# Tree attention on one core: transposes one pair ahead at first, V copies spread by pairs, loads in another order

## The chip, the cores and the metric

The kernel runs on one NeuronCore of a Trainium2 chip. The metric is the device time of one execution in microseconds (us); smaller is better. The core's engines run at the same time, each through its own instructions in order: TensorE (PE, matmuls and transposes; PEld is its weight load), VectorE (DVE), ScalarE (ACT), GpSimd (POOL) and SyncE (SP). Data moves between the device memory (HBM) and the on-chip memory by DMAs, which one of the engines issues and which 16 DMA engines then carry out.

## The reference

```python
def setup_inputs():
    batch, heads, seq, dim = 8, 12, 512, 64          # Q, K, V: float32, random normal
...
def reference(Q, K, V):
    scale = 1.0 / np.sqrt(dim)
    mask = np.zeros((seq, seq))
    for i in range(seq):                 # a row attends to itself and its ancestors
        mask[i, i] = 1                   # in a binary heap
        parent = i
        while parent > 0:
            parent = (parent - 1) // 2
            mask[i, parent] = 1
    scores = np.einsum('bhqd,bhkd->bhqk', Q, K) * scale
    scores = scores + (1 - mask) * (-1e9)
    weights = np.exp(scores - np.max(scores, axis=-1, keepdims=True))
    weights = weights / (np.sum(weights, axis=-1, keepdims=True) + 1e-10)
    return np.einsum('bhqk,bhkd->bhqd', weights, V).astype(np.float32)
```

Batch and heads are taken together: 96 heads of 512 rows by 64 columns.

## The kernel before

Heads are worked on in pairs, 48 of them (pair i is heads 2i and 2i+1), and loaded in groups of 8 heads (12 groups, four pairs each). Row 4p+t of a head lies in partition p, slot t.

**One pair.** `transpose(i)` (L254) turns the pair's K and Q by 16 matmuls into one PSUM tile `kqp`, of which there is a single buffer. `evac(i)` (L267) copies it to `kq` on DVE, a pair's K and Q side by side. `scores1` (L283) and `scores2` (L305) each add a mask code to the scores by matmuls over `ctile` and then multiply keys and queries from `kq`; ACT takes the exponential of each (L298, L321). `values(i)` (L337) multiplies the weights with V from the tile `vt`, into a single PSUM buffer `ob`, with a column of ones that gives the sums. `norm(i)` (L369) takes the reciprocal of the sums and multiplies, both on DVE, into `of`.

**V copies.** `values` needs V in an order of rows that follows the tree. Three kinds of copies bring it from the loaded tile `vst` into `vt`, all recorded at L209: `spread_l7` on DVE (32 partitions, two slots), `spread_top` (32 partitions, one slot) on POOL, for the first four heads on DVE, and `spread_leaves` (64 partitions, two slots) on ACT or POOL. A group takes 4 + 4 + 2 of them; early groups are taken by halves of 4 heads. `early_copies(i)` is the table of what is copied at step i up to 11; from 12 on, the group after the current one is copied, one `spread_l7` and a share of the others per step. `spread(i)` issues them, and from step 6 on makes the first POOL copy behind a DVE copy of the same step wait for that DVE copy (`after`, L390).

**Loads.** All loads but the first pair's K and Q are issued by POOL (L189), in its program order, between its copies; they read float32 and write bfloat16. `loads_at(i)` says which are issued after step i's copies: eleven before the loop, then those of its table, and from step 13 on three in four steps. The K and Q tiles and the V tiles have four buffers each, one per group in flight. A DMA issued by POOL counts on one of eight semaphores by turns, and the compiled program makes a DMA wait until the one eight places before it has landed. Stores of finished groups (1 MB, L385) are issued by POOL from step 33 on, one a step, the last group's in three pieces.

**The order of the steps** is written out by hand in the loop at L496; no scheduler moves anything. At step i PE does the scores of pair i, then `values(i - 1)`, then the transposes of pair i+2 (`AHEAD` makes exceptions of steps 1 to 3, where two pairs are transposed at once or none). Before the loop stand eight matmuls over zeros (`fill`), the first pair's transposes and scores, five more `fill` matmuls, the second pair's transposes, the copies of the first four heads' V and `values(0)`.

Of the kernel before, what the change touches and what calls it, by code (L numbers as in the profile page):

```python
# [98 lines left out]
def kernel(  # L99
# [12 lines left out]
    NH = B * H  # L112
    NP = NH // 2
# [100 lines left out]
    def spread_top(eng, j, g, h0=0, h1=GB):  # L214
        return copy(
            eng, vtile(g)[32 * j:32 * j + 32, h0:h1, 0, 0:D],
            vsts[g][0:32, h0:h1, UNITS[TOP + j][1], :],
        )

    def spread_leaves(eng, r, g, h0=0, h1=GB):  # L220

        p = 64 if r else 0
        return copy(
            eng, vtile(g)[p:p + 64, h0:h1, 1 + r:4 + r:2, 0:D],
            vsts[g][64:128, h0:h1, r:3 + r:2, :],
        )
# [27 lines left out]
    def transpose(i):  # L254
        kqp = psT.tile([P, 2, 32, 32], bf16, name="kqp")
        kqps[i] = kqp
        for t in range(4):
            for a in range(2):
                transpose_one(kqp[:, 0, :, :], i, a, t, _slot_layout(t)[1], ksts, perms[t])
        for x, t in enumerate(ORDER):  # L260
            for a in range(2):
                transpose_one(
                    kqp[:, 1, :, :], i, a, t, [2 * x, 2 * x + 1, 2 * x + 9, 2 * x + 10],
                    qsts, qperm,
                )

    def evac(i):  # L267
        kq = work.tile([P, 2, 16, 32], bf16, name="kq")
        kTs[i] = kq[:, 0, :, :]
        qTs[i] = kq[:, 1, :, :].rearrange("p (t u) c -> p t (u c)", t=4)  # L270
        src = kqps[i][:, :, 0:18, :]
        src = bass.AP(
            src.tensor, src.offset,
            [list(src.ap[0]), [1024, 2], [32, 8], [9 * 32, 2], [1, 32]],
        )
        nc.vector.tensor_copy(  # L276
            out=kq[:, :, :, :].rearrange("p k (x y) c -> p k x y c", y=2), in_=src
        )
# [48 lines left out]
    def fill(i, n):  # L327

        if i not in obs:
            obs[i] = psO.tile([P, 2, 512], fp32, name="ob")  # L330
        for k in range(n):
            nc.tensor.matmul(
                out=obs[i][:, k % 2, :], lhsT=zeros[:, 0:128], rhs=zeros[:, :],
                start=True, stop=True,
            )

    def values(i):  # L337

        if i == NP - 1:
            obs[i] = psT.tile([P, 2, 512], fp32, name="kqp")  # L340
        elif i not in obs:
            obs[i] = psO.tile([P, 2, 512], fp32, name="ob")
        ob = obs[i]
        e1, e2, vt = ets[i], e2s[i % NE], vtile(2 * i // GB)

        def product(e, a, t, tile_v, lo=0, hi=128, **flags):
            nc.tensor.matmul(  # L347
                out=ob[lo:hi, a, 65 * t:65 * t + 65],
                lhsT=e[:, a, PLACE[t], lo:hi],
                rhs=vt[:, 2 * i % GB + a, tile_v, 0:D + 1],  # L350
                **flags,
            )

        def first(a):
            for t in range(4):
                product(e1, a, t, 0, start=t == 0, stop=False)
            for t in (2, 3):
                product(e2, a, t, 1 + t, start=False, stop=False)

        def second(a):  # L360
            for t in (0, 1):
                product(e2, a, t, 1 + SELF[t], 0, 64, start=False, stop=t == 1)
                product(e2, a, t, 1 + t, 64, 128, start=False, stop=t == 1)

        order = (first, second) * 2 if i == NP - 1 else (first, first, second, second)
        for n, part in enumerate(order):
            part(n // 2 if i == NP - 1 else n % 2)

    def norm(i, heads=((0, 2),)):  # L369
        g, r = divmod(i, 4)  # L370
        if r == 0:
            ofs[g] = opool.tile([P, GB, 4, D], fp32, name="of")
        for a0, a1 in heads:
            o4 = obs[i][:, a0:a1, 0:260].rearrange("p a (t c) -> p a t c", c=D + 1)
            rec = small.tile([P, a1 - a0, 4, 1], fp32, name="rec")
            nc.vector.reciprocal(out=rec[:, :, :, :], in_=o4[:, :, :, D:D + 1])  # L376
            nc.vector.tensor_tensor(  # L377
                out=ofs[g][:, 2 * r + a0:2 * r + a1, :, :],
                in0=o4[:, :, :, 0:D],
                in1=rec[:, :, :, :].to_broadcast([P, a1 - a0, 4, D]),  # L380
                op=ALU.mult,
            )
# [15 lines left out]

    def early_copies(i):

        def l7(g, js, *h):
            return [(spread_l7, DVE, j, g) + h for j in js]

        def top(g, js, *h):
            return [(spread_top, POOL, j, g) + h for j in js]

        def leaf(eng, g, rs, *h):
            return [(spread_leaves, eng, r, g) + h for r in rs]

        every = range(4)  # L410
        return {
            0: l7(0, every, 0, 4) + [(spread_top, DVE, j, 0, 0, 4) for j in every]
            + leaf(ACT, 0, (0, 1), 0, 4),
            1: l7(0, every, 4, 8) + top(0, every, 4, 8) + leaf(ACT, 0, (0, 1), 4, 8),
            3: l7(1, every, 0, 4) + top(1, every, 0, 4) + leaf(ACT, 1, (0, 1), 0, 4),
            5: l7(1, every, 4, 8) + top(1, every, 4, 8) + leaf(ACT, 1, (0, 1), 4, 8),
            6: l7(2, (0,)) + top(2, (0, 1)) + leaf(ACT, 2, (0,)),
            7: l7(2, (1, 2)) + top(2, (2, 3)) + leaf(ACT, 2, (1,)),
            8: l7(2, (3,)),
            9: l7(3, (0,)) + top(3, (0, 1)),  # L420
            10: l7(3, (1, 2)) + top(3, (2, 3)) + leaf(ACT, 3, (1,)),
            11: l7(3, (3,)) + leaf(POOL, 3, (0,)),
        }.get(i, [])

    def spread(i):

        g, j = i // 4 + 1, i % 4
        if i < 12:
            todo = early_copies(i)
        elif g < NG:  # L430
            todo = [(spread_l7, DVE, j, g)]
            if j < 2:
                todo += [(spread_top, POOL, k, g) for k in (2 * j, 2 * j + 1)]
            else:
                todo += [(spread_leaves, POOL, j - 2, g)]
        else:
            todo = []
        last = None
        for f, eng, *args in todo:
            done = f(eng, *args)  # L440
            if eng is DVE:
                last = done
            elif eng is POOL and i >= 6 and last is not None:
                after(done, last)
                last = None

    def loads_at(i):

        k4 = lambda h: [(load_k, h, 4), (load_q, h, 4)]
        start = [(load_v, 0, 4), (load_k, 2, 2), (load_q, 2, 2)] + k4(4) + [(load_v, 4, 4)]  # L450
        start += k4(8) + [(load_v, 8, 4)] + k4(12)
        early = {
            -1: start, 1: [(load_v, 12, 4), (load_v, 16), (load_k, 16)], 2: [(load_q, 16)],
            3: [(load_v, 24), (load_k, 24)],
            5: [(load_q, 24), (load_v, 32), (load_k, 32), (load_q, 32)],
            9: [(load_v, 40)], 10: [(load_k, 40)],
            11: [(load_q, 40), (load_v, 48)], 12: [(load_k, 48), (load_q, 48)],
        }
        if i in early:
            return early[i]  # L460
        g, j = i // 4 + 3, i % 4
        if i < 13:
            return []
        if j == 0:
            return [(load_q, GB * g)] if g < NG else []
        if j < 3 and g + 1 < NG:
            return [((load_v, load_k)[j - 1], GB * (g + 1))]
        return []

    stored = []  # L470

    def pool(i):
        for f, *args in loads_at(i):
            f(*args)
        if i >= 33:
            for g in range(len(stored), min((i - 4) // 4, NG - 2) + 1):
                if len(stored) < i - 32:
                    stored.append(g)
                    store(g)

    AHEAD = {1: (2, 3), 2: (), 3: (4, 5)}

    pool(-1)
    fill(0, 8)
# [2 lines left out]
    evac(0)  # L487
    scores1(0)
    scores2(0)
    fill(0, 5)  # L490
    transpose(1)
    spread(0)
    evac(1)
    values(0)
    norm(0)
    for i in range(1, NP + 1):  # L496
        if i < NP:
            scores1(i)
            scores2(i)
        if i >= 2:  # L500
            values(i - 1)
            norm(i - 1, ((0, 1), (1, 2)) if i == NP else ((0, 2),))
        for n in AHEAD.get(i, (i + 2,)):
            if n < NP:
                transpose(n)
                evac(n)
        spread(i)
        pool(i)
        if i == NP - 2:
            store(NG - 1, 0, 4)  # L510
# [32 lines left out]
```

## Time and profile before

| | us |
|---|---|
| median of the three runs | 138.5 |
| lowest and highest | 137.82, 138.73 |
| profiled execution, its own time | 137.91 |
| its span in the trace | 136.2 |
| PE, DVE, ACT, POOL busy | 116.5, 102.8, 92.5, 93.1 |

The profile's page and the trace are of that one execution, taken on the chip. The span reaches from the first to the last event on record; the execution's own time is 1.7 us longer. Busy time counts an engine's instructions, overlaps merged. Two rows of the page split the span into 40 slices: a digit is a share in tenths. The timeline lists runs of like instructions by engine: start, busy time, engine, line, tile written and read, count, and in brackets how long the engine had been idle before, and what ended that. "Issue to landing" of a DMA is the time from its issue by an engine until the last of the 16 DMA engines has written its part.

### The profile page before, as it was taken

Reading aid. Unit: us, or ns where it says so; the run is one execution under the profiler, and the core shown is the slowest. Engines: PE = TensorE matmul, PEld = TensorE weight load, DVE = VectorE, ACT = ScalarE, POOL = GpSimd, SP = SyncE. Lnnn points to the kernel's source line nnn. Section 1 sums busy time; section 2 is a strip of 40 time slices with the busy share of each in tenths; the row PEclk is TensorE's granted clock in tenths of the full one; section 3 lists DMA queues with packets and bytes.
Section 4 is the critical chain, followed back from the end, with each engine's and each line's share of the span. In section 5 each row is a group of like instructions: output and inputs, shape, how many; then the busy total and the mean of one; then the engine's idle time right before and its main releaser. Section 6 shows DMA issues by size and latency. Waiting matters only on the chain.

```text
span 136.2 us, 5474 instructions
## 1 busy us (share of the span) xinstructions
PE 116.5 (86%) x2413; PEld 81.0 (60%) x2413; DVE 102.8 (75%) x215; ACT 92.5 (68%) x110; POOL 93.1 (68%) x129
## 2 busy tenths in 40 slices
PE   6899859989898997999999798989989499979900
PEld 2336546757576775777676576767667376757500
DVE  2485766698799999899879777988989567785530
ACT  4174983799989777578686586868686456757700
POOL 6973999703356999786996776767888755781240
PEclk9999995999999999999999999999999959999995
DMA  4999999999999999999999999999999999999971
GB/s 115 226 189 195 197 196 198 199 197 199 202 194 200 197 200 197 198 197 198 197 199 200 195 199 197 198 198 198 202 306 406 401 402 394 402 390 398 375 303 48
DMA packets 41082, 32.34 MB, mean 238 GB/s; under 512 B 954, under 2 KB 37946, under 8 KB 41058
## 3 DMA queue, kind: packets, MB, share of 16 engines
q0 software_dynamic: 40320, 31.20, 125.2%
q1 hardware_dynamic: 466, 0.53, 1.2%
q8 instruction: 19, 0.31, 0.8%
q10 hardware_dynamic: 272, 0.26, 0.6%
q14 instruction: 5, 0.04, 0.1%
HBM read 38.01 MB, written 12.58 MB: 372 GB/s over the span
## 4 chain that ended last, share of the span: by engine, by line
PE 47%; DMA 15%; POOL 14%; issue 12%; DVE 5%; ACT 3%; POOLq 1%; ACTq 0%
PE ob L347 16%; PE kqp L250 10%; DMA qst<-in_Q_dram 9%; PE s L287 7%; DMA vst<-in_V_dram 5%; PE s L316 5%; PE s L292 5%; PE s L310 5%; POOL vt L209 5%; POOL vst L189 3%; POOL qst L189 2%; POOL kst L189 2%; DVE vt L209 2%; POOL out_dram L385 2%; DVE of L377 2%
## 5 line engine op out<-in xcount | busy, mean ns | idle before, releaser
L298 ACT ACTIVATE e<-s 128x1024 bf16<-128x1024 f32 x48 | 49.2, 1024 | 32.9 <-PE s L292 32.5
L209 POOL COPY vt<-vst 32x512 bf16<-32x512 bf16 (+2 forms) x69 | 46.7, 676 | 30.8 <-DVE vt L209 24.0
L347 PE MATMUL ob<-vt,e 128*128 128x65 bf16 (+1 forms) x940 | 38.3, 198 | 2.6 <-DVE of L377 1.2
L321 ACT ACTIVATE e<-s 128x768 bf16<-128x768 f32 x48 | 38.6, 805 | 0.1
L276 DVE COPY kq<-kqp 128x1024 bf16<-128x1024 bf16 x48 | 32.8, 683 | 6.2 <-PE kqp L250 6.1
L347 PEld LDWEIGHTS <-e 128*128 128x128 bf16 (+1 forms) x960 | 31.0, 103 | 10.8 <-issue 1.8
L377 DVE TENSOR_TENSOR of<-ob,rec 128x512 f32<-128x512 f32 x47 | 32.5, 691 | 1.6
L209 DVE COPY vt<-vst 32x1024 bf16<-32x1024 bf16 (+2 forms) x60 | 28.2, 470 | 1.7 <-DMA vst<-in_V_dram 0.2
L250 PE MATMUL kqp<-ptile,kst 128*64 128x128 bf16 x384 | 20.1, 225 | 4.9 <-issue 2.6
L250 PE MATMUL kqp<-ptile,qst 128*64 128x128 bf16 x384 | 19.9, 225 | 1.4 <-issue 1.0
L316 PEld LDWEIGHTS <-kq 64*128 64x128 bf16 x384 | 14.9, 96 | 9.5 <-issue 2.7
L287 PE MATMUL s<-ctile 40*128 40x512 bf16 x96 | 19.4, 399 | 0.8 <-ACT e L298 0.7
L376 DVE RECIPROCAL rec<-ob 128x8 f32<-128x8 f32 x47 | 9.7, 207 | 13.8 <-PE ob L347 12.0
L292 PE MATMUL s<-kq 64*128 64x512 bf16 x96 | 19.0, 390 | 0.6 <-issue 0.4
L316 PE MATMUL s<-kq 64*128 64x64 bf16 (+1 forms) x384 | 18.4, 213 | 0.7 <-issue 0.7
L310 PE MATMUL s<-ctile 40*128 40x480 bf16 x96 | 18.3, 377 | 0.5
L250 PEld LDWEIGHTS <-kst 128*64 128x64 bf16 x384 | 13.5, 113 | 7.1 <-issue 6.1
L385 POOL DMA_DIRECT2D out_dram<-of x14 | 12.0, 854 | 6.6 <-DVE of L377 6.6
L250 PEld LDWEIGHTS <-qst 128*64 128x64 bf16 x384 | 14.4, 114 | 1.7 <-issue 1.1
L189 POOL DMA_DIRECT2D vst<-in_V_dram x14 | 12.1, 865 | 0.9 <-POOLq L527 0.8
L310 PEld LDWEIGHTS <-ctile 40*128 40x128 bf16 x96 | 7.3, 97 | 8.7 <-issue 2.5
L189 POOL DMA_DIRECT2D qst<-in_Q_dram x14 | 12.2, 872 | 0.0
(22 smaller groups left out, 44.3 us busy)
## 6 DMA issues: line engine op xcount, KB each, us to landing
out_dram<-of POOLq DMA_DIRECT2D x11, 1024.0 KB, 9.5
vst<-in_V_dram POOLq DMA_DIRECT2D x10, 512.0 KB, 12.3
kst<-in_K_dram POOLq DMA_DIRECT2D x10, 512.0 KB, 12.9
qst<-in_Q_dram POOLq DMA_DIRECT2D x10, 512.0 KB, 12.4
vst<-in_V_dram POOLq DMA_DIRECT2D x4, 256.0 KB, 7.2
kst<-in_K_dram POOLq DMA_DIRECT2D x3, 256.0 KB, 8.0
qst<-in_Q_dram POOLq DMA_DIRECT2D x3, 256.0 KB, 8.6
out_dram<-of POOLq DMA_DIRECT2D x1, 512.0 KB, 6.0
```

Of the source, the lines that this page charges most:

```text
L189: nc.gpsimd.dma_start(out=kept[g][:, h0 % GB:h0 % GB + n, :, :].rearrange("p h t d -> p h (t d)"), in_=src[:, h0:h0 + n, :],)
L209: return (eng.copy if eng is nc.scalar else eng.tensor_copy)(out=out, in_=in_)
L250: nc.tensor.transpose(out=dst, in_=st[2 * i // GB][:, 2 * i % GB + a, t, :], identity=perm)
L276: nc.vector.tensor_copy(out=kq[:, :, :, :].rearrange("p k (x y) c -> p k x y c", y=2), in_=src)
L287: nc.tensor.matmul(out=sp[:, a, :], lhsT=k1code[64 * a:64 * a + BITS, :], rhs=q1code[64 * a:64 * a + BITS, :], start=True, stop=False,)
L292: nc.tensor.matmul(out=sp[:, a, :], lhsT=keys(i, a, TOP), rhs=qTs[i][64 * a:64 * a + 64, :, :].rearrange("p t c -> p (t c)"), start=False, ...
L298: nc.scalar.activation(out=et[:, :, :, :].rearrange("p a t c -> p (a t c)"), in_=sp[:, :, :].rearrange("p a c -> p (a c)"), func=AF.Exp, s ...
L310: nc.tensor.matmul(out=flat[:, a, 32:512], lhsT=k2code[64 * a:64 * a + BITS, :], rhs=q2code[64 * a:64 * a + BITS, 32:512], start=True, sto ...
L316: nc.tensor.matmul(out=flat[:, a, lo:hi], lhsT=keys(i, a, TILE2[t]), rhs=qTs[i][64 * a:64 * a + 64, :, :].rearrange("p t c -> p (t c)")[:, ...
L321: nc.scalar.activation(out=e2s[i % NE][:, :, :, 32:128].rearrange("p a t c -> p (a t) c"), in_=sp[:, :, :, 32:128].rearrange("p a t c -> p ...
L347: nc.tensor.matmul(out=ob[lo:hi, a, 65 * t:65 * t + 65], lhsT=e[:, a, PLACE[t], lo:hi], rhs=vt[:, 2 * i % GB + a, tile_v, 0:D + 1], **flags,)
L377: nc.vector.tensor_tensor(out=ofs[g][:, 2 * r + a0:2 * r + a1, :, :], in0=o4[:, :, :, 0:D], in1=rec[:, :, :, :].to_broadcast([P, a1 - a0, ...
```

## The change

Three things are changed, all of them in the order of instructions; the loop's arithmetic and all tiles stay.

- **TensorE.** `ready(n)` is `transpose(n)` and `evac(n)`, `finish(i)` is `values(i)` and `norm(i)`. Up to step 9 (`TURN`) the transposes of pair i+1 stand between the scores of pair i and `values(i - 1)`; at step 9 pairs 10 and 11 are both transposed, and from then on the order is the old one. The start is written anew: two `fill` matmuls in place of five, and the scores of pair 1 ahead of `values(0)`.
- **V copies.** The table of `early_copies` is spread: the second half of group 0 partly before the loop and partly at step 2, the halves of group 1 over steps 3 to 6, group 2 over steps 7 and 8, group 3 over 9 to 11 as before. One `spread_leaves` of each of these goes to POOL instead of ACT (group 3's already did). The wait of a POOL copy for a DVE copy begins at step 9 instead of 6.
- **Loads.** `plan()` makes one sequence. V of heads 12 to 15 moves ahead of the loop. K and Q of heads 16 to 39 are loaded by halves of four heads, in the order K16, Q16, V16 (8 heads), K20, Q20, V24 (8), K24, Q24, K28, Q28, K32, Q32, V32 (8), K36, Q36. From head 40 on a group is loaded in the order K, Q, V. How many are issued after which step is in `counts`; from step 13 on it is one a step. There are 48 loads instead of 42, of the same bytes in all.

```diff
-            0: l7(0, every, 0, 4) + [(spread_top, DVE, j, 0, 0, 4) for j in every]
-            + leaf(ACT, 0, (0, 1), 0, 4),
-            1: l7(0, every, 4, 8) + top(0, every, 4, 8) + leaf(ACT, 0, (0, 1), 4, 8),
-            3: l7(1, every, 0, 4) + top(1, every, 0, 4) + leaf(ACT, 1, (0, 1), 0, 4),
-            5: l7(1, every, 4, 8) + top(1, every, 4, 8) + leaf(ACT, 1, (0, 1), 4, 8),
-            6: l7(2, (0,)) + top(2, (0, 1)) + leaf(ACT, 2, (0,)),
-            7: l7(2, (1, 2)) + top(2, (2, 3)) + leaf(ACT, 2, (1,)),
-            8: l7(2, (3,)),
-            9: l7(3, (0,)) + top(3, (0, 1)),
-            10: l7(3, (1, 2)) + top(3, (2, 3)) + leaf(ACT, 3, (1,)),
-            11: l7(3, (3,)) + leaf(POOL, 3, (0,)),
+            2: part(0, range(4), (), (), (), 4, 8),
+            3: part(1, (0, 1), (0, 1), (0,), (), 0, 4),
+            4: part(1, (2, 3), (2, 3), (), (1,), 0, 4),
+            5: part(1, (0, 1), (0, 1), (0,), (), 4, 8),
+            6: part(1, (2, 3), (2, 3), (), (1,), 4, 8),
+            7: part(2, (0, 1), (0, 1), (0,)),
+            8: part(2, (2, 3), (2, 3), (), (1,)),
+            9: part(3, (0,), (0, 1)),
+            10: part(3, (1, 2), (2, 3), (1,)),
+            11: part(3, (3,), (), (), (0,)),
...
-            elif eng is POOL and i >= 6 and last is not None:
+            elif eng is POOL and i >= 9 and last is not None:
...
-        start = [(load_v, 0, 4), (load_k, 2, 2), (load_q, 2, 2)] + k4(4) + [(load_v, 4, 4)]
-        start += k4(8) + [(load_v, 8, 4)] + k4(12)
-        early = {
-            -1: start, 1: [(load_v, 12, 4), (load_v, 16), (load_k, 16)], 2: [(load_q, 16)],
-            3: [(load_v, 24), (load_k, 24)],
-            5: [(load_q, 24), (load_v, 32), (load_k, 32), (load_q, 32)],
-            9: [(load_v, 40)], 10: [(load_k, 40)],
-            11: [(load_q, 40), (load_v, 48)], 12: [(load_k, 48), (load_q, 48)],
-        }
...
+        seq = [(load_v, 0, 4), (load_k, 2, 2), (load_q, 2, 2)]
+        for h in (4, 8, 12):
+            seq += k4(h) + [(load_v, h, 4)]
+        seq += k4(16) + [(load_v, 16)] + k4(20) + [(load_v, 24)] + k4(24) + k4(28)
+        seq += k4(32) + [(load_v, 32)] + k4(36)
+        for h in range(40, NH, GB):
+            seq += [(load_k, h), (load_q, h), (load_v, h)]
+        counts = {-1: 12, 1: 2, 3: 1, 4: 2, 5: 1, 6: 2, 7: 1, 8: 2, 9: 1, 10: 2, 11: 1, 12: 2}
+        at = {}
+        for i in range(-1, 33):
+            n = counts.get(i, 1 if i > 12 else 0)
+            at[i], seq = seq[:n], seq[n:]
...
-    AHEAD = {1: (2, 3), 2: (), 3: (4, 5)}
+    def ready(n):
+        if n < NP:
+            transpose(n)
+            evac(n)
+
+    def finish(i):
+        values(i)
+        norm(i, ((0, 1), (1, 2)) if i == NP - 1 else ((0, 2),))
+
+    TURN = 9
...
-    fill(0, 5)
+    for r in range(2):
+        spread_leaves(ACT, r, 0, 0, 4)
     transpose(1)
-    spread(0)
+    for j in range(4):
+        spread_top(DVE, j, 0, 0, 4)
     evac(1)
-    values(0)
-    norm(0)
-    for i in range(1, NP + 1):
+    fill(0, 2)
+    for j in range(4):
+        spread_l7(DVE, j, 0, 0, 4)
+    scores1(1)
+    scores2(1)
+    finish(0)
+    for j in range(4):
+        spread_top(POOL, j, 0, 4, 8)
+    spread_leaves(ACT, 0, 0, 4, 8)
+    spread_leaves(POOL, 1, 0, 4, 8)
+    ready(2)
+    finish(1)
+    pool(1)
+    for i in range(2, NP + 1):
         if i < NP:
             scores1(i)
             scores2(i)
-        if i >= 2:
-            values(i - 1)
-            norm(i - 1, ((0, 1), (1, 2)) if i == NP else ((0, 2),))
-        for n in AHEAD.get(i, (i + 2,)):
-            if n < NP:
-                transpose(n)
-                evac(n)
+        if i <= TURN:
+            ready(i + 1)
+        if i > 2:
+            finish(i - 1)
+        if i >= TURN:
+            ready(i + 2)
```

More of the change, by code (lines that the diff above doesn't have):

```diff
@@ L399, in early_copies, with part @@
     def early_copies(i):
[L401 to L410, printed above, removed]
-        return {
-            0: l7(0, every, 0, 4) + [(spread_top, DVE, j, 0, 0, 4) for j in every]
-            + leaf(ACT, 0, (0, 1), 0, 4),
-            1: l7(0, every, 4, 8) + top(0, every, 4, 8) + leaf(ACT, 0, (0, 1), 4, 8),
-            3: l7(1, every, 0, 4) + top(1, every, 0, 4) + leaf(ACT, 1, (0, 1), 0, 4),
-            5: l7(1, every, 4, 8) + top(1, every, 4, 8) + leaf(ACT, 1, (0, 1), 4, 8),
-            6: l7(2, (0,)) + top(2, (0, 1)) + leaf(ACT, 2, (0,)),
-            7: l7(2, (1, 2)) + top(2, (2, 3)) + leaf(ACT, 2, (1,)),
-            8: l7(2, (3,)),
-            9: l7(3, (0,)) + top(3, (0, 1)),
-            10: l7(3, (1, 2)) + top(3, (2, 3)) + leaf(ACT, 3, (1,)),
-            11: l7(3, (3,)) + leaf(POOL, 3, (0,)),
+        def part(g, l7=(), top=(), acts=(), pools=(), *h):
+            return (
+                [(spread_l7, DVE, j, g) + h for j in l7]
+                + [(spread_top, POOL, j, g) + h for j in top]
+                + [(spread_leaves, ACT, r, g) + h for r in acts]
+                + [(spread_leaves, POOL, r, g) + h for r in pools]
+            )
+        return {
+            2: part(0, range(4), (), (), (), 4, 8),
[8 more added lines that the diff above has]
+            11: part(3, (3,), (), (), (0,)),
         }.get(i, [])
@@ L442, in spread, with plan @@
                 last = done
-            elif eng is POOL and i >= 6 and last is not None:
+            elif eng is POOL and i >= 9 and last is not None:
                 after(done, last)
                 last = None
-    def loads_at(i):
+    def plan():
         k4 = lambda h: [(load_k, h, 4), (load_q, h, 4)]
-        start = [(load_v, 0, 4), (load_k, 2, 2), (load_q, 2, 2)] + k4(4) + [(load_v, 4, 4)]
-        start += k4(8) + [(load_v, 8, 4)] + k4(12)
-        early = {
-            -1: start, 1: [(load_v, 12, 4), (load_v, 16), (load_k, 16)], 2: [(load_q, 16)],
-            3: [(load_v, 24), (load_k, 24)],
-            5: [(load_q, 24), (load_v, 32), (load_k, 32), (load_q, 32)],
-            9: [(load_v, 40)], 10: [(load_k, 40)],
-            11: [(load_q, 40), (load_v, 48)], 12: [(load_k, 48), (load_q, 48)],
-        }
[L459 to L468, printed above, removed]
+        seq = [(load_v, 0, 4), (load_k, 2, 2), (load_q, 2, 2)]
[10 more added lines that the diff above has]
+            at[i], seq = seq[:n], seq[n:]
+        assert not seq
+        return at
+    LOADS = plan()
     stored = []
     def pool(i):
-        for f, *args in loads_at(i):
+        for f, *args in LOADS.get(i, ()):
             f(*args)
```

## The prediction

> **What bounds the kernel now.** I read the page's slices first, then the DMA issues with their times to landing, then POOL's timeline, then the groups on DVE.
>
> ```profile
> DMA  4999999999999999999999999999999999999971
> GB/s 115 226 189 195 197 196 198 199 197 199 202 194 200 197 200 197 198 197 198 197 199 200 195 199 197 198 198 198 202 306 406 401 402 394 402 390 398 375 303 48
> ```
>
> The DMA row is full from the second slice to the 38th, at two steady rates: 198 GB/s of bfloat16 written while loading, 400 while storing. By bytes: loads 18.9 MB / 198 = 95 us, stores 12.6 MB / 400 = 31 us, 126 of the 136.2 us. The queue of transfers, not an engine, sets the end. The DMA issues between 24 and 27 us show how full it is, and the trace's last store what it costs when it is not:
>
> ```profile
> vst<-in_V_dram POOLq DMA_DIRECT2D x1, 512.0 KB, 16.2
> kst<-in_K_dram POOLq DMA_DIRECT2D x1, 512.0 KB, 18.0
> qst<-in_Q_dram POOLq DMA_DIRECT2D x1, 512.0 KB, 20.1
> ```
> ```profile
> DMA to landing us min/median/max: 3.6/3.6/3.6
> ```
>
> V32, K32 and Q32 (heads 32 to 39), issued at 23.86, 24.72 and 25.58, land at 40.1, 42.7 and 45.7: 2.65 us apart (512 KB at 198 GB/s), behind a backlog of 16 us and more. The last store, 256 KB issued at 131.07, lands 3.6 us later; 0.65 is moving (256 KB at 400), so 2.95 us lie between an issue and data that find no queue. POOL's timeline shows what the backlog is for:
>
> ```profile
> 25.58 0.90 POOL L189 DMA_DIRECT2D qst<-in_Q_dram  x1
> ...
> 31.32 1.25 POOL L209 COPY vt<-vst 32x512 bf16<-32x512 bf16 x2 [4.83 <-DVE vt L209]
> ...
> 38.81 1.25 POOL L209 COPY vt<-vst 32x512 bf16<-32x512 bf16 x2 [3.65 <-DVE vt L209]
> ...
> 40.02 0.88 POOL L189 DMA_DIRECT2D vst<-in_V_dram  x1
> ```
>
> Between 25.6 and 40 us POOL issues no load: its copies wait for DVE copies of the same step. The queue lives on what was issued before; V40, issued at 40.02, still finds 5.7 us of it.
>
> PE takes 2.11 us a pair when nothing is missing (exponentials start at 56.75, 58.86, 60.97), but is behind from the start: pair 5's exponential starts at 25.4, where 7.63 + 5 x 2.11 would be 18.2.
>
> **The change, part by part.**
>
> *Bytes and count of loads.* The bytes stay. Six loads are split: six more issues of 0.87 us (Q loads in the part of the page on groups) are 5.2 us of POOL. In the queue a split costs nothing: the halves at the start land 1.3 us apart, two of them 2.65.
>
> *Start and transposes.* Three `fill` matmuls of 0.43 us go and pair 1's scores precede `values(0)`. Walked by durations of the timeline: `evac(1)` ends at 10.2, four `spread_l7` of 0.39 at 11.7, `values(0)` follows; `evac(2)` ends at 14.1, `evac(3)` at 16.5, the four copies of heads 4 to 7 at 18.0, when `values(2)` starts. From there one step a pair, on DVE:
>
> ```profile
> L276 DVE COPY kq<-kqp 128x1024 bf16<-128x1024 bf16 x48 | 32.8, 683 | 6.2 <-PE kqp L250 6.1
> L377 DVE TENSOR_TENSOR of<-ob,rec 128x512 f32<-128x512 f32 x47 | 32.5, 691 | 1.6
> L376 DVE RECIPROCAL rec<-ob 128x8 f32<-128x8 f32 x47 | 9.7, 207 | 13.8 <-PE ob L347 12.0
> ```
>
> 0.68 + 0.69 + 0.21 and two `spread_l7`, 0.35 each for 4 heads, 0.53 for 8 (the groups of L209 on DVE by shape): 2.3 to 2.6 us, over PE's 2.11; I take 2.4. Six steps lead from 18.0 to `values(8)` at 32.5. Step 9 then has on DVE the rest of `values(8)`'s normalization (to 34.2), `evac(11)` (34.9) and the first copy of heads 24 to 31 (35.4). Before, that copy stood at 38.3: PE's part gains 3 us, and the wait for Q16 at 29.27 (0.5 us) goes, since half of Q lands earlier. That gain is worth nothing by itself: the queue carries the same bytes.
>
> *Copies moved from ACT to POOL.* Four `spread_leaves`: three halves of 0.6 (ACT's half copy 0.61) and one of 1.04, 2.9 us on POOL. With the splits POOL has 8 us more before step 9 and 8.5 us of idle time there (4.83 + 3.65). Walked copy by copy from the landing of V4 at 12.5, it issues K32 about 2 us before the queue gets to it; covered, at nothing. That cover ends at step 9.
>
> *Loads, the dear part.* Q16 landed at 29.2 (16.65 + 12.6). The bytes up to there are now those up to Q20. Behind it come V24 (2.65) and K24, Q24, K28, Q28, K32 (1.33 each): the queue is empty at **38.5**. K32 is issued at step 8; Q32 stands behind step 9's two POOL copies, the first of which waits for the DVE copy of 35.4.
> - Q32: copies to 36.7 (1.25), issue, landing after 2.95 + 1.33 at 41.0; without a break 39.8. **Lost 1.2.**
> - V32: one step later, behind step 10's copies, at 39.3; landing 2.95 + 2.65 later at 44.9 instead of 43.7. **Lost 1.2.** K36 and Q36 close up, to 47.5.
> - K40 stands behind step 12's POOL copies, which need V32 landed, on DVE too: 44.9 + 0.5 + 1.25 = 46.7; landing 52.3 instead of 50.2. **Lost 2.1.**
> - From there one load of 2.65 us a step of 2.1 to 2.4: the queue fills again.
>
> Sum 4.5 us, if DVE copies beside POOL copies run at their shortest. They have no order before step 9 now, and beside a POOL copy a `spread_l7` of 8 heads took 0.75 (at 49.96) against 0.42. By the mean rows, with PE's waits for instructions ("issue"), I put step 9 1.0 us later, all of it in Q32's loss: **5.5 us**. Bounds: 4.5, with only the last two losses 3.3, and 7.5 if all overlapped copies take 0.75 and TensorE's clock drops as it did at 20.5 us (half of full speed for 3.4 us, at most 1.7 lost).
>
> *What is late next.* DVE waits in order for V32 at step 12 and for V40 at step 16; V40 lands at about 58.6 (K40 at 53.3, Q40 and V40 behind it) where DVE copied it at 54.96. Compute ends some 3.6 us later, the last store would land at 134.7 + 3.6 = 138.3; the queue ends at 134.7 + 5.5 = 140.2. The queue decides.
>
> The sum: 137.9 + 5.5 = 143.4 for the profiled execution; the median of the runs lies 0.6 above it, so **144.0**.
>
> TensorE's clock was at half for 3.4 us from 20.5 us, after PE waits of 0.5 and 1.18 us, and from 109.2, after one of 1.77. The Trainium skill ("TensorE: Matmul & The Clock Gate", What's actually happening) lets the clock fall only after about 3.4 us idle; by it, an estimate, only the wait for V40 would do it, by the rows both V waits; compute would end 1.7 or 3.4 us later still, so the end 144.0 or, with 3.4, about 145.5.
>
> **The rivals.**
>
> *Not slower, rather faster:* the lag of the slowest DMA engine shrinks. In the landings of the trace the last of the 16 engines is 1.5 us behind the first at 20 us, 2.8 from 70 on and 3.8 from 121 on; both jumps stand beside PE waits for instructions (70.3, 121). If the 3 us gained on PE keep step 9 ahead of 33 us, no break occurs, and if the new positions avoid the second of those jumps the end is 1 us earlier, both 2: 136.5. It decides only where the queue never runs dry. Against it: the gate at step 12 holds however fast PE is. The Trainium skill ("DMA: Bandwidth & Descriptors", Latency and other measured facts) says two of the DMA engines are usually slower; by it the lag is there to stay, and this case ends at 138.5. Four in a hundred.
>
> *No change:* the breaks are filled by the slowest engine, which at 40 us is 1.8 us behind, and step 9 comes 2 us earlier than walked: 138.5 to 139.8. Nine.
>
> *Worse:* step 9 comes 3 us or more late, because PE stalls again at the start (as at 20.57, 1.18 us, for `evac`) with the clock at half, and compute, not the queue, ends last after both V waits: 3.6 + 2 x 1.7 and late copies, 8 to 11 us, 147 to 150. Twenty.
>
> *As worked out:* 142 to 146.5. Sixty-seven. That a load stands elsewhere than the text says is excluded: the order is by hand and the instructions stand so.
>
> **The numbers.** About 1% (1.4 us) is what a measurement of this kernel can tell from no change. Slower 0.67 + 0.20 = 0.87, same 0.09, faster 0.04. The range from 140.5 to 149 leaves out no change and faster (0.13) and the far end of the worse case (0.05).
>
> **What would show it.** Right: slices of the DMA row under 9 and under 190 GB/s between 36 and 53 us; POOL's copy of step 9 waiting on DVE until 35 to 37 us, with a Q load issued just after and landing about 4.3 us later; DVE waiting on V loads at steps 12 and 16, 3 to 5 us each; stores landing some 5 us later. Wrong: a DMA row of nines throughout, or K40 issued before V32 has landed.

## The result and the profile after

| | before | changed |
|---|---|---|
| median of four runs, us | 138.62 | 146.94 |
| lowest and highest | 137.82, 139.35 | 144.91, 147.56 |
| profiled execution, its span | 137.91, 136.2 | 144.91, 142.6 |

The ratio of the changed kernel to the one before is 1.055, 95% interval 1.043 to 1.068: slower by 4 to 7%. Here and below a ratio and its interval go by the runs within 1.5% of the fastest of their kernel, a median by all of them. The profiled execution is the fastest of the four; a fifth run of the same kernel (below) took 144.73.

The slices of the page, changed kernel; 3.57 us each, DMA in tenths of full:

```profile
DMA  4999999999979799999999999999999999999990
GB/s 127 215 189 197 197 195 198 201 193 197 139 84 195 72 187 199 196 174 158 193 198 197 198 199 197 198 197 198 200 202 374 403 402 402 398 404 399 402 358 38
```

The row that stood at 198 GB/s while loading now has holes: 139 and 84 in slices 11 and 12 (35.7 to 42.8 us), 72 in slice 14 (46.3 to 49.9), 174 and 158 in slices 18 and 19 (60.6 to 67.7). Before and after them the two rates are the old ones. POOL's timeline, changed kernel, shows what stands at the holes:

```profile
32.34 0.75 POOL L189 DMA_DIRECT2D kst<-in_K_dram  x1
35.37 1.25 POOL L209 COPY vt<-vst 32x512 bf16<-32x512 bf16 x2 [2.27 <-DVE vt L209]
36.57 0.74 POOL L189 DMA_DIRECT2D qst<-in_Q_dram  x1
38.17 1.27 POOL L209 COPY vt<-vst 32x512 bf16<-32x512 bf16 x2 [0.86 <-DVE vt L209]
39.40 0.89 POOL L189 DMA_DIRECT2D vst<-in_V_dram  x1
...
42.06 0.74 POOL L189 DMA_DIRECT2D qst<-in_Q_dram  x1
45.97 1.27 POOL L209 COPY vt<-vst 32x512 bf16<-32x512 bf16 x2 [3.17 <-DVE rec L376]
47.19 1.03 POOL L189 DMA_DIRECT2D kst<-in_K_dram  x1
...
59.73 1.27 POOL L209 COPY vt<-vst 32x512 bf16<-32x512 bf16 x2 [4.29 <-DVE vt L209]
60.95 1.09 POOL L189 DMA_DIRECT2D vst<-in_V_dram  x1
```

The loads in these rows are K32, Q32, V32, Q36, K40 and V48. Each of Q32, V32, K40 and V48 stands behind a pair of V copies, which wait for DVE. And DVE waits for the V load that was issued late, at step 12 and again at step 16 (DVE's timeline, changed kernel):

```profile
45.43 0.42 DVE L209 COPY vt<-vst 32x1024 bf16<-32x1024 bf16 x1 [3.33 <-DMA vst<-in_V_dram]
...
59.25 0.41 DVE L209 COPY vt<-vst 32x1024 bf16<-32x1024 bf16 x1 [4.23 <-DMA vst<-in_V_dram]
```

At the end the stores queue: the last one, issued at 133.0, lands 8.2 us later, where before it took 3.6 (times to landing of the stores, changed kernel). The engines are done; the transfers are not.

```profile
DMA to landing us min/median/max: 8.2/12.7/14.6
```

**The breaks, read from the landings.** The first of the 16 DMA engines to finish a load gives a clean cadence: 1.33 us for a load of four heads, 2.65 for eight, while the queue is full. What a landing is late beyond that is a break.

| load | first engine lands, us | break |
|---|---|---|
| K32 | 37.24 | |
| Q32 | 40.10 | 1.53 |
| V32 | 44.70 | 1.95 |
| K36, Q36 | 46.06, 47.36 | 0 |
| K40 | 52.67 | 2.66 |
| Q40 to Q48 | 55.30 to 63.30 | 0 |
| V48, K56, Q56 | 66.54, 69.49, 72.24 | 0.59, 0.30, 0.10 |

Together 7.1 us. The last load's first landing moves from 99.43 to 106.78 (7.35), the last store's landing from 134.66 to 141.24 (6.6).

### The profile page after: what moved, and what is told of

Read it like the earlier page. It is cut to its first block, busy times and chain, and to the rows that moved or that the text cites. A ratio compares the mean times of both kernels' runs of the same rounds, so it can differ in the third digit from the quotient of the medians.

```text
span 142.6 us, 5476 instructions
## 1 busy us (share of the span) xinstructions
PE 115.1 (81%) x2409; PEld 80.6 (57%) x2410; DVE 103.2 (72%) x215; ACT 89.8 (63%) x106; POOL 99.8 (70%) x139
## 2 busy tenths in 40 slices
DMA packets 41178, 32.34 MB, mean 227 GB/s; under 512 B 1050, under 2 KB 38042, under 8 KB 41154
## 4 chain that ended last, share of the span: by engine, by line
PE 36%; POOL 20%; DMA 17%; issue 13%; DVE 7%; POOLq 1%
DMA vst<-in_V_dram 17%; PE ob L347 13%; POOL vt L209 8%; PE kqp L250 7%; PE s L287 5%; POOL kst L189 4%; POOL qst L189 4%; PE s L292 4%; PE s L310 3%; PE s L316 3%; DVE of L377 2%; POOL vst L189 2%; DVE vt L209 2%; POOL out_dram L385 2%; DVE kq L276 1%
## 5 line engine op out<-in xcount | busy, mean ns | idle before, releaser
L209 POOL COPY vt<-vst 32x512 bf16<-32x512 bf16 (+3 forms) x73 | 49.7, 680 | 25.6 <-DVE vt L209 16.5
L347 PE MATMUL ob<-vt,e 128*128 128x65 bf16 (+1 forms) x940 | 39.0, 199 | 9.5 <-DVE of L377 7.2
L347 PEld LDWEIGHTS <-e 128*128 128x128 bf16 (+1 forms) x960 | 31.5, 104 | 17.8 <-DVE of L377 7.0
L316 PEld LDWEIGHTS <-kq 64*128 64x128 bf16 x384 | 14.5, 94 | 9.3 <-issue 1.6
L316 PE MATMUL s<-kq 64*128 64x64 bf16 (+1 forms) x384 | 17.7, 208 | 0.5 <-issue 0.5
L189 POOL DMA_DIRECT2D kst<-in_K_dram x17 | 14.1, 832 | 0.0
L189 POOL DMA_DIRECT2D qst<-in_Q_dram x17 | 14.0, 822 | 0.0
## 6 DMA issues: line engine op xcount, KB each, us to landing
out_dram<-of POOLq DMA_DIRECT2D x1, 512.0 KB, 10.6
```

The costliest lines, as they stand in the source:

```text
L189: nc.gpsimd.dma_start(out=kept[g][:, h0 % GB:h0 % GB + n, :, :].rearrange("p h t d -> p h (t d)"), in_=src[:, h0:h0 + n, :],)
L209: return (eng.copy if eng is nc.scalar else eng.tensor_copy)(out=out, in_=in_)
L316: nc.tensor.matmul(out=flat[:, a, lo:hi], lhsT=keys(i, a, TILE2[t]), rhs=qTs[i][64 * a:64 * a + 64, :, :].rearrange("p t c -> p (t c)")[:, ...
L347: nc.tensor.matmul(out=ob[lo:hi, a, 65 * t:65 * t + 65], lhsT=e[:, a, PLACE[t], lo:hi], rhs=vt[:, 2 * i % GB + a, tile_v, 0:D + 1], **flags,)
```

## The experiments

All figures beside "before" are against runs of the kernel before on the same chip.

**Which of the three parts.** Two kernels exchange the loads only.

```diff
 changed kernel, loads of before:
-        for f, *args in LOADS.get(i, ()):
+        for f, *args in loads_at(i):
 kernel before, loads of the change:
-        for f, *args in loads_at(i):
+        for f, *args in LOADS.get(i, ()):
```

> The changed kernel with the loads of before (order, sizes and steps of issue); transposes one pair ahead and the new spread of V copies stay. Theory (the loss is a transfer queue that runs dry because loads are issued too late): the queue stays full, no slice of the DMA row under 9 until the last stores, time as before, 137.5 to 139.5 us. Rival (the new order of transposes and copies costs the time by itself): it stays near the changed kernel, 144 to 147 us.

Measured: median 139.01 us, before 137.85; ratio 1.005 (1.000 to 1.010).

> The kernel before with only the new loads; transposes, copies and the wait of POOL copies for DVE copies from step 6 on stay as before. Theory: the same late issue, and worse, since POOL reaches steps 6 to 9 later (its copies waited until 31.3 and 38.8 us there): K24 and Q24 only after 32.6 us, Q32 at about 40; 8 to 14 us over before, 146 to 152 us, with several gaps in the DMA row between 30 and 55 us. Rival: 138 to 140 us.

Measured: median 146.98 us, ratio 1.067 (1.054 to 1.079). Its slices, new loads in the kernel before:

```profile
DMA  4999999979999699999999999999999999999981
GB/s 138 214 194 193 197 196 198 196 90 169 169 128 187 94 162 196 192 194 140 179 198 198 198 199 197 198 198 198 201 204 360 406 397 406 398 402 399 404 325 47
```

So the loads are the whole loss. With the old ones the new transposes and copies neither gain nor lose more than a percent; with the new ones the old kernel is as slow as the changed one, and its holes begin earlier (slice 9, from 29 us), as step 6's copies wait for DVE there:

```profile
29.43 1.25 POOL L209 COPY vt<-vst 32x512 bf16<-32x512 bf16 x2 [5.62 <-DVE vt L209]
```

**Order and halves, or when they are issued.** The sequence of loads is kept, and only the steps of issue move: one step earlier from step 3 on, or one step later from Q28 on.

```diff
-        counts = {-1: 12, 1: 2, 3: 1, 4: 2, 5: 1, 6: 2, 7: 1, 8: 2, 9: 1, 10: 2, 11: 1, 12: 2}
 earlier:
+        counts = {-1: 12, 1: 2, 3: 2, 4: 2, 5: 2, 6: 2, 7: 2, 8: 1, 9: 2, 10: 2, 11: 1, 12: 2,
+                  20: 0, 24: 0, 28: 0}
 later:
+        counts = {-1: 12, 1: 2, 3: 1, 4: 2, 5: 1, 6: 2, 7: 1, 8: 0, 9: 2, 10: 1, 11: 2, 12: 1, 13: 2}
```

> The changed kernel with the same sequence of loads, halves included, each issued about one step earlier from step 3 on (K20 at step 3, V32 at 8, K40 and Q40 at 10, V40 at 11, K48 and Q48 at 12; none at steps 20, 24 and 28, where a buffer is not yet free). Theory: what counts is how much has been issued by each step, not the order and not the halves: no gap in the DMA row before the stores, 137.5 to 139.5 us, the whole loss back. Rival (the order K, Q, V or the copies cost something by themselves): 141 or more.

Measured: median 138.6 us, before 139.6; ratio 1.002 (0.996 to 1.008). The whole loss is back, with the same order and the same halves. The slices, loads one step earlier:

```profile
DMA  3999999999999999999999999999999999999960
GB/s 98 248 190 196 196 196 198 196 198 196 198 200 177 182 200 196 197 201 196 198 197 199 198 198 198 199 200 196 199 308 397 403 401 403 401 403 395 404 263 30
```

Only slices 13 and 14 (177, 182) are a little low: K40 still lands 0.7 us late. POOL's copies of step 9 stand at 37.44 there, 2.1 us later than in the changed kernel (35.37), and the queue holds out all the same.

> The changed kernel with its loads from Q28 on issued one step later (Q28 and K32 at step 9, Q32 at 10, V32 and K36 at 11, Q36 at 12, K40 and Q40 at 13, then one a step): the suspected cause doubled. Theory: each step later costs the queue about one step of the engines, and V32 lands later for step 12's copies, which wait longer: K40 lands 3 to 5.5 us later than in the changed kernel; 148 to 152 us. Rival (the time is set elsewhere): within 1.5 us of the changed kernel.

Measured: median 156.27 us (154.23 to 158.46), before 138.5; the profiled execution 154.23, against 144.91. The direction is right, the size too small: 9.3 us more in the profiled executions, where 3 to 5.5 were expected for K40 and 148 to 152 in all. K40 does land 5.2 us later (57.87; the long breaks before it are 3.7 us at Q28 and 4.9 at Q36), but V40 and V48 then come late for steps 16 and 20 and hold POOL there too (6.24 and 2.82 us, and 3.4 of break at Q48): the last load is 10.1 us later than in the changed kernel.

**Single breaks.** Three kernels take away one cause each.

```diff
 Q32 and V32 at step 8:
-        counts = {... 8: 2, 9: 1, 10: 2, 11: 1, 12: 2}
+        counts = {... 8: 4, 9: 1, 10: 1, 11: 1, 12: 2}
 no order of copies at steps 9 and 10:
-            elif eng is POOL and i >= 9 and last is not None:
+            elif eng is POOL and i >= 11 and last is not None:
 K40 and Q40 ahead of step 12's copies:
-        spread(i)
-        pool(i)
+        if i == 12:
+            pool(i)
+            spread(i)
+        else:
+            spread(i)
+            pool(i)
```

> The changed kernel with Q32 and V32 issued at the end of step 8, right behind K32, instead of at steps 9 and 10 (K36 and Q36 one step earlier too, all later loads one place ahead). Theory: Q32 and V32 follow K32 without a break, V32 has landed by about 43 us, so that neither K40's issue at step 11 nor the copies of step 12 wait for it; of 6.6 us lost 6 come back, 138 to 140 us. If only the break at K40 counted, or the halves of K and Q cost the queue something by themselves, 142 to 145.

Measured: median 142.32 us, ratio 1.030 (1.020 to 1.040). Nearly half of the loss is back, not all. Q32 and V32 follow without a break (38.77, 41.43), and step 12 waits for no load. But Q36 (45.30) is 1.1 us late and K40 (49.20) 1.25; POOL's timeline, this kernel:

```profile
34.02 0.91 POOL L189 DMA_DIRECT2D vst<-in_V_dram  x1
37.98 1.25 POOL L209 COPY vt<-vst 32x512 bf16<-32x512 bf16 x2 [3.04 <-DVE vt L209]
39.18 0.76 POOL L189 DMA_DIRECT2D kst<-in_K_dram  x1
```

Step 9 came at 37.98, 2.6 us later than in the changed kernel (35.37), and Q36 and K40, still at steps 10 and 11, are now the loads that come late. The edit did not make step 9 late. Up to the loads of step 8 the two programs are the same, and the engines of this execution were 1.4 us behind at pair 2 (its exponential starts at 15.62, not 14.19) and 2.7 at pair 9 (33.43, not 30.70). DVE's copies of step 8, then the first of step 9, in the changed kernel:

```profile
31.02 1.56 DVE L209 COPY vt<-vst 32x1024 bf16<-32x1024 bf16 x2
...
34.89 0.41 DVE L209 COPY vt<-vst 32x1024 bf16<-32x1024 bf16 x1
```

and in this one:

```profile
33.75 1.44 DVE L209 COPY vt<-vst 32x1024 bf16<-32x1024 bf16 x2
...
37.50 0.41 DVE L209 COPY vt<-vst 32x1024 bf16<-32x1024 bf16 x1
```

So the run shows the break passing to the next late load; what the two loads give back when step 9 comes at 35.4 it does not show.

> The changed kernel with one wait fewer: at steps 9 and 10 POOL copies no longer wait for the DVE copy of the same step (they write other partitions). Theory: POOL issues Q32 at about 34.4 and V32 at about 36.5 us, both before the queue gets there, so their two breaks (1.5 and 2.0 us on the fast DMA engines) go; K40 still stands behind copies that need V32 landed (about 43), a break of about 2 us stays, and V48's of 0.9. 3 to 4 us come back: 140.5 to 143.5 us.

Measured: median 144.07 us, ratio 1.045 (1.033 to 1.057); the profiled execution 143.74. 1.2 us are back in the profiled execution where 3 to 4 were expected. Here is the reason (POOL's timeline, without the order):

```profile
33.68 0.74 POOL L189 DMA_DIRECT2D qst<-in_Q_dram  x1
34.46 1.27 POOL L209 COPY vt<-vst 32x512 bf16<-32x512 bf16 x2
35.68 0.88 POOL L189 DMA_DIRECT2D vst<-in_V_dram  x1
36.55 0.76 POOL L189 DMA_DIRECT2D kst<-in_K_dram  x1
41.68 1.03 POOL L209 COPY vt<-vst 64x1024 bf16<-64x1024 bf16 x1 [4.37 <-DVE vt L209]
42.66 0.74 POOL L189 DMA_DIRECT2D qst<-in_Q_dram  x1
```

Q32 and V32 go out early, as expected, and their breaks are gone (0 and 0.2 us). POOL then waits at step 11 for DVE, 4.37 us, and the break of 2.5 us is at Q36. K40's stays, as expected (1.9), and V48's too (1.4, where 0.9 was expected). How much has been issued by the time the engines reach step 11 is unchanged, so the queue runs dry about as long, one load further on. Here too a part is not the edit's: this execution was 1.75 us behind the changed kernel's at pair 9 (32.45 against 30.70).

> The changed kernel with K40 and Q40 issued ahead of step 12's V copies instead of behind them; nothing else. Those copies wait for V32 to land (45.4 us). Theory: K40 is issued at about 42.8 right behind Q36, its break of 2.7 us goes, V40 lands about 2.7 us earlier and V48's break of 0.9 goes with it: 3 to 3.6 us back, a profiled execution near 141.5 (144.9 in the changed kernel) and a median of 142 to 144. If breaks only move to the next late load: under 1 us back.

Measured: median 144.04 us, ratio 1.039 (1.029 to 1.049); the profiled execution 142.88. K40's break falls from 2.66 to 0.2 us, as expected, and Q32's and V32's stay (1.4, 2.2). Of the 3 to 3.6 us expected, 2.0 come back in the profiled execution: V48, K56 and Q56 are now 0.8, 0.45 and 0.5 us late, since step 16 is still held by V40. Part comes back, part moves.

**Do halves cost the queue?**

```diff
-            5: [(load_q, 24), (load_v, 32), (load_k, 32), (load_q, 32)],
+            5: [(load_q, 24, 4), (load_q, 28, 4), (load_v, 32), (load_k, 32, 4), (load_k, 36, 4),
+                (load_q, 32, 4), (load_q, 36, 4)],
 and likewise K and Q of heads 16 to 31 at steps 1, 2 and 3
```

> The kernel before with only the K and Q loads of heads 16 to 39 split into halves of four heads, issued back to back where the whole ones were: 48 loads for 42, same bytes, same order. Theory (a split costs the queue nothing): 137.5 to 139.5 us and a full DMA row. POOL must wait in step 5 for the DMA eight places before (Q36 for K24, about 33 us), so its copies of step 6 come some 2 us later; that is expected to hide, since the queue then holds 10 us of loads. Rival (each split has a fixed price in the queue, or the limit of eight DMAs in flight starves it): 141 us or more, with gaps in the DMA row.

Measured: median 140.33 us, before 139.6; ratio 1.017 (1.004 to 1.029). Between the two expectations. In the queue the halves cost nothing: from V32 on (38.56) they land at 39.91, 41.23, 42.57, 43.91, 1.34 us apart. On POOL they do cost (timeline, kernel before with halves; the bracket ends with the engine the profile names, but the compiled instruction also waits for the DMA eight places before; the six issues of step 5 before which POOL stands idle come 0.3 to 0.6 us after that one has landed):

```profile
32.89 0.88 POOL L189 DMA_DIRECT2D qst<-in_Q_dram  x1 [2.12 <-PE s L292]
33.98 0.74 POOL L189 DMA_DIRECT2D qst<-in_Q_dram  x1 [0.21 <-issue]
...
40.63 1.25 POOL L209 COPY vt<-vst 32x512 bf16<-32x512 bf16 x2 [3.21 <-DVE vt L209]
41.84 0.88 POOL L189 DMA_DIRECT2D vst<-in_V_dram  x1
44.37 1.25 POOL L209 COPY vt<-vst 32x512 bf16<-32x512 bf16 x2 [1.66 <-DVE vt L209]
45.58 0.88 POOL L189 DMA_DIRECT2D kst<-in_K_dram  x1
```

With eight DMAs in flight at most, eight halves are 10.6 us of backlog where eight whole loads are 21. POOL ends step 5 at 34.7 and not at 26.5: 4.5 of these 8.2 us are such waits, the rest mostly the issues that the halves add. Step 6's copies and all after them come later, and V40 and K40 (0.4 and 1.2 us) find the queue dry.

**What the engines gained.** In both kernels below the stores of groups 0 to 10 are left out, so that the end is set by the engines.

```diff
                     stored.append(g)
-                    store(g)
```

> The kernel before without the stores of groups 0 to 10 (only the last group is written; all else is computed and loaded as before), so that after the loads the queue is empty and the end is set by the engines. Theory: before, queue and engines end together (last normalization 130.8, last store landed 134.7), so the time hardly falls: 136 to 138 us. Rival (the stores alone set the end of before): well under 134.

Measured: median 133.64 us (131.63 to 134.99), ratio 0.956 (0.944 to 0.967): some 6 us faster, where at most 2.5 were expected. The queue is only a part of that, for without the stores the engines are faster too: from pair 38's normalization to pair 46's they take 16.9 us, 2.1 a pair, and with the stores 21.6. In that stretch PE stands waiting for nothing that the profile shows (PE's timeline, kernel before):

```profile
108.17 0.41 PE L250 MATMUL kqp<-ptile,kst 128*64 128x128 bf16 x7 [1.77 <-issue]
```

From 95 us on these waits come to 3.6 us, without the stores to 0.8. How much of the 6 us is queue and how much engines, the run does not tell apart.

> The version with loads issued one step earlier, likewise without the stores of groups 0 to 10. Theory: transposes one pair ahead and the new spread of copies do gain some 3 us on the engines (last normalization 127.9 against 130.8 us), which the queue hides: without the stores 133 to 135.5 us, 2 to 3 us under the same cut of the kernel before. Rival (they gain nothing, the engines are paced by something else): the same as that cut, within 1 us.

Measured: median 130.33 us (129.81 to 131.29), under the 133 to 135.5 expected. The ratios to the uncut kernel are 0.956 (0.944 to 0.967) and 0.942 (0.935 to 0.949): 1.9 us apart, with intervals that just meet. So the gain on the engines is likely some 2 us, not shown clear of the noise, and it is that of all three parts of this version together, its earlier loads included. With the stores in place nothing of it is left (1.005 and 1.002 above).

**The changed kernel once more.**

> The changed kernel once more, one look, because its profiled execution (144.9 us) is 2 us under the other three of its runs. Theory: the same three breaks in the queue and one more or longer one, where PE waits for instructions or for its clock before step 9 or step 12; 144.5 to 147 us, with step 9's POOL copies later than 35.4 us in the slower case. If the queue breaks are the same to 0.3 us and the time is over 146, the 2 us come from something else, such as a longer lag of the slowest DMA engine at the end.

Measured: 144.73 us, with breaks of 1.0, 2.1, 2.8 and 1.4 us at Q32, V32, K40 and from V48 on. Both profiled executions agree; why the others took some 2 us more was not caught by either and stays open. One candidate is on record: in both of these, step 9 came early. Pair 9's exponential starts at 30.70 and 30.26, and in two of the three versions above that are the same program up to step 8's loads at 33.43 and 32.45 (30.46 in the third). A run of the changed kernel with step 9 that late would lose more at Q32; none was traced.

**A version that might beat both.**

```diff
-        nc.gpsimd.dma_start(
+        nc.sync.dma_start(
             out=Or[:, GB * g + h0:GB * g + h0 + n, :],
```

> The version with loads issued one step earlier, with all stores issued by SyncE instead of GpSimd, at the same places of the program. There the engines end at 127.9 us and the slowest DMA engine 4.2 us behind the first, at 135.5. If that lag comes with POOL's queue, it shrinks and the time falls to 135 to 137.5 us, under both kernels; if it comes from what that engine carries, the time stays at 138 to 139.5.

Measured: median 154.86 us, ratio 1.116 (1.106 to 1.126). The edit did more than it was meant to. POOL's program order is what kept the stores behind the loads; SyncE has nothing in front of them, and issues a group's store as soon as it is normalized (times of the stores, and the issues between 20 and 60 us with their times to landing, stores on SyncE):

```profile
L385 SPq DMA_DIRECT2D out_dram<-of x14: 372/372/393, 23.4 to 151.0; - x14
```
```profile
out_dram<-of SPq DMA_DIRECT2D x4, 1024.0 KB, 11.4
vst<-in_V_dram POOLq DMA_DIRECT2D x4, 512.0 KB, 17.9
kst<-in_K_dram POOLq DMA_DIRECT2D x3, 512.0 KB, 18.4
```

The first store goes out at 23.4 us, and the loads now have the stores beside them. DVE waits 25.8 us for V loads in all. The lag of the slowest DMA engine, which the run was meant for, was not tested by it and stays open; no version beat the kernel before.

## Why the prediction was right, and where it was off

**The mechanism held step by step.** Landings by the last DMA engine, as the prediction counted them, without and with the 1.0 us that it added for a late step 9:

| | predicted, us | with 1.0 added | measured |
|---|---|---|---|
| first DVE copy of step 9 ends | 35.4 | 36.4 | 35.30 |
| Q32 landed (issued at 36.57 for 36.7) | 41.0 | 42.0 | 40.97 |
| V32 landed (issued at 39.40 for 39.3) | 44.9 | 45.9 | 45.41 |
| K40 landed | 52.3 | 53.3 | 53.22 |
| V40 landed | 57.6 | 58.6 | 59.23 |
| last store landed | 139.2 | 140.2 | 141.24 |

The signs that it named are there too: the holes between 36 and 53 us, POOL's copy of step 9 waiting for DVE until 35.37, Q32 landing 4.4 us after its issue, and DVE's waits of 3.33 and 4.23 us at steps 12 and 16. What bounds the kernel was read rightly: the queue. The loads alone make the loss, all of it comes back when they are issued earlier, and across the kernels the time follows the last load:

| kernel (profiled execution) | last load lands later than before, us | time later |
|---|---|---|
| loads one step earlier | 0.9 | 1.3 |
| before, with halves | 3.0 | 2.4 |
| Q32, V32 at step 8 | 3.3 | 4.4 |
| K40 ahead of the copies | 5.3 | 5.0 |
| no order at 9 and 10 | 6.5 | 5.8 |
| changed | 7.35 | 7.0 |
| before, with the new loads | 8.7 | 8.6 |
| loads one step later | 17.4 | 16.3 |

(First landing of the last load against 99.43; time against 137.91. The executions are from several chips.)

**The sum was 1.1 us short in the profiled execution.** It had 5.5; the queue ended 6.6 later. Counted where both kernels have moved the same bytes, again by the last DMA engine:

| up to | changed, us | before, us | later | predicted |
|---|---|---|---|---|
| Q36 (before: Q32) | 49.11 | 45.66 | 3.45 | 3.4 |
| V40 (before: Q40) | 59.23 | 53.39 | 5.84 | 5.5 |
| V48 (before: Q48) | 68.08 | 61.31 | 6.77 | 5.5 |
| last store | 141.24 | 134.66 | 6.6 | 5.5 |

- *The 3.4 was met by luck.* It is 2.4 for Q32 and V32 and 1.0 for a late step 9, and step 9 was not late. The two loads lost more by themselves. The prediction sized their breaks at 1.2 us each on the last DMA engine, but the first one runs out of work earlier (K32 lands at 37.24 there, at 38.89 on the last), and on it the breaks are 1.53 and 1.95.
- *The 2.95 us "between an issue and data that find no queue" was too small.* It was read from the last store, whose slowest DMA engine still had the store before it to finish (134.02, 0.64 us ahead of 134.66), so it was not the price of an empty queue. V32 and K40 took 6.0 us each from issue to landing, not 5.6: 3.4 in place of 2.95.
- *"From there one load ... a step: the queue fills again" left out a break.* At step 16 POOL waited for V40, as DVE did, and V48 went out at 60.95, behind it: 0.9 us from V48 on, for which the prediction had no term, though it had seen the wait itself ("DVE waits in order for V32 at step 12 and for V40 at step 16"). It counted that wait for the engines only, and the loads stand behind the same copies.

The walk to step 9 was met by luck too: 35.4 against 35.30. The six steps between were right (14.3 us for 14.5), but `values(2)` began at 17.20 and not at 18.0, and `values(8)` then stood 0.84 us for the copies of step 8, which were slow beside POOL's (1.56 us for two). That slowing is what the added 1.0 us was for, and it differs from one execution to the next: the two copies of step 7 took 0.94 us here, and 1.60 in both versions above with a late step 9. On the median (146.94 against 144.0) another 2 us are unexplained.

**"In the queue a split costs nothing"** was right there, and wrong as a whole: halving alone cost 1.7% (0.4 to 2.9) in the kernel before, by way of POOL: the limit of eight DMAs and the added issues. In the changed kernel this limit does not bite where the breaks are, since the issue comes late anyway (Q32 goes out at 36.57; the DMA eight places before it, K20, landed at 28.19).

**The copies moved to POOL at nothing** were covered, as said: K32 was issued at 32.34 and the queue got to it about 35.9, when Q28 landed. **The gain on the engines** was sized at 3 us at step 9, and is there: the first copy of that step starts at 34.89 where it stood at 38.34. At the end, without the stores, some 2 us of gain are likely (above). "That gain is worth nothing by itself" was right too.

**The rivals.** "Faster" needed the queue never to run dry: with the loads earlier, it did so for only 0.7 us, and still the time stayed at 1.002, as the slowest DMA engine was 4.2 us behind at the end, not less. "Worse" expected the engines to end last; they ended at 132.7 (the last DVE instruction), the queue 8.5 later. The median, 146.94, lies just above the range of the case "as worked out" (142 to 146.5), but the traces show that case and not the worse one. The clock did fall to half twice before the end, from 46.65 and from 60.3 us, 3.4 us each, as PE waits of 2.54 and 3.84 us were ending (PE's timeline, changed kernel):

```profile
46.74 1.20 PE L347 MATMUL ob<-vt,e 128*128 128x65 bf16 x20 [2.54 <-DVE of L377]
...
60.56 1.20 PE L347 MATMUL ob<-vt,e 128*128 128x65 bf16 x20 [3.84 <-DVE of L377]
```

The Trainium skill ("TensorE: Matmul & The Clock Gate", What's actually happening) would have the clock fall after about 3.4 us idle; the first of these waits is shorter, so the rows held, and the rule did not. Hidden behind the queue, it cost nothing that the end shows.

## What to carry to other kernels

When the transfers are the bound, ask of every load how much is still queued when it is issued, and which copies and waits stand before it on the issuing engine: here the order of the loads and the speed of the engines mattered only through that. A wait removed upstream can move the break to the next late load unless the whole issue moves earlier. And splitting loads shortens the backlog wherever the number of DMAs in flight, not their bytes, is limited.

## What the runs showed of the hardware that was not expected

- The 16 DMA engines drift apart. The slowest was 0.8 us behind the first on landings at 10 us and 3.8 behind at 125 in the kernel before; after the three long breaks of the changed kernel the lag is back at 0.5 to 0.9 us (K40: 52.67 first, 53.22 last), and so gives back a little of what the break cost: 7.35 us at the last load became 6.6 at the end.
- Stores issued by another engine share the DMA engines with the loads at once. With stores on SyncE, V loads of 512 KB issued between 20 and 60 us took 14.4 to 20.4 us to land (9.6 to 15.3 with the stores on POOL), with 1 MB stores landing after 11.4 beside them. The Trainium skill ("DMA: Bandwidth & Descriptors", Issuing engines are not separate DMA queues) says that DMAs run on the same 16 engines and interleave, whoever issues them; the rows agree.
- Stores slowed the engines, not only the queue. From 95 us on PE's waits for nothing that the profile shows fell from 3.6 to 0.8 us when eleven of the twelve groups' stores were left out, and from 2.8 to 0.5 in the version with the loads one step earlier. How a store makes PE wait stays open.
